# Two layers of a hybrid diffusion backbone on one core: activation slots and weight pieces that begin at other byte addresses

## The chip, the cores and the metric

One Trainium2 chip, one of its cores. The metric is the device time of one execution, in microseconds. The kernel before was run twice without a profile: 3562.77 and 3561.64 us, median 3562.2 us. One more execution was profiled; all durations below come from that one.

## The reference, cut to what matters

A latent stream x (1024 tokens, 1024 features) and a context prefix (256 tokens) go through two layers. Each layer does the following, in float32:

```
h  = modulate(rms_norm(x, g1), shift, scale)        # per token norm, per feature affine
qkv = h @ w_in                                      # 1024 -> three head groups A, B, C
o  = attention of the groups A (GQA), B (window), C (differential)
x  = x + gate1 * (o @ w_out)
h2 = modulate(rms_norm(x, g2), shift2, scale2)
u, g = split(dwconv3(h2 @ w_up))                    # 1024 -> 2 x 2816
x  = x + gate2 * ((silu(g) * u) @ w_down)
```

The context tokens take the same path with modulations of their own; the second layer computes only what the latent stream needs.

## The kernel before, in words

**Layout.** Features lie on the 128 partitions, tokens along the free dimension: 1280 tokens (1024 latent, 256 context) of a 128-feature block are one slot of 1280 float32 values, 5120 bytes per partition. There are eight blocks (KT = 8).

**Pairs of high and low parts.** Every large product is made of operands split in two: a high part, rounded to the format `fp32r` that TensorE takes in one pass (written `hh`, `ah`, `wh`, `iph`), and a low part, the rest (`hl`, `al`, `wl`, `ipl`). A product is three matmuls: high by high, high by low, low by high. `split` (L102 to L104) makes a pair: a cast on ACT and a subtraction on DVE.

**Slots.** One pool lives through the whole program: eight slots `x0` to `x7` for the residual stream and sixteen slots `hh0, hl0` to `hh7, hl7` for the normalised activations. `slot` (L295) hands them out by name. Two of them, `x7` and `hl7`, are eight values wider than used. Pools place tiles one behind the other, so the program as it is built puts `hh0` at byte 57504 of the partition and each further `h` slot 5120 bytes on; the weight pieces `w` of the FFN begin at byte 143008 and then every 4096. All sixteen `h` slots and all weight pieces so begin at 160 modulo 256; the `x` slots begin at 128 modulo 256. Every column offset that a matmul takes in them is a multiple of 512 bytes, or of 256 bytes in the windowed attention, so no moving operand of the program begins off a multiple of 32 bytes.

**Stages of a layer.**
- *Modulation* (`ada`, L170): `w_ada` streamed through free slots as the moving operand, 128x512 pieces. In the first layer the first piece goes through the `h` slots, later ones through the `x` slots.
- *First norm* (L241 to L278): the scaled input is cast to `hh` on ACT (L278), and `hl` is made on DVE (L267) or POOL (L264).
- *Input projection* (`inproj`, L398): here the `h` slots are the stationary operand, 128 tokens at a time, and the pieces `iph`, `ipl` of `w_in` are the moving operand, 384 wide. 60 steps of 24 matmuls.
- *Attention* (`attention`): the `h` slots are free then and hold queries, keys and bias tables. ACT or POOL write the high part (L585, L587), DVE or POOL the low part (L594). Scores (L672) read them as both operands. A list scheduler, `Sched`, sets the order at build time by costs that stand in the code; byte addresses do not enter it. The probabilities `P` are transposed (L776) and multiplied by the values (L795).
- *Output projection* (L927) and second norm: stationary are the pieces of `w_out`, moving are the `h` slots, 512 or 256 tokens at a time. The first three pieces of `w_out` lie in the FFN's weight buffers.
- *FFN*: up projection (`mm`, L991), stationary `w` (128 of the 1024 values of a piece), moving `hh` or `hl`, in chunks of 512, 512 and 256 tokens in the first layer and twice 512 in the second; down projection (`down_mm`, L1078), stationary `w`, moving the activation tiles `ah`, `al`. The weights come through `Stream`: the raw piece by DMA, split into a pair of tiles from `tiles` (L1499), three pairs in rotation (`n_hi` = 3).

Matmuls of these four products, by their lines: 2880 (L398), 1152 (L927), 5280 (L991), 2640 (L1078); the scores (L672) are 1536.

Of the kernel before, what the change touches and what calls it, by code (L numbers as in the profile page):

```python
# [15 lines left out]
F32R = mybir.dt.float32r  # L16
# [6 lines left out]
L, D, T, NL, NC = 2, 1024, 1280, 1024, 256  # L23
# [50 lines left out]
class Build:  # L74
# [218 lines left out]


    def slot(self, s, dt=F32):  # L295
        w = T + 8 if s in ("x7", "hl7") else T
        return self.sl[1].tile([128, w], dt, name=self.name(s), tag=s, bufs=1)[:, :T]

    def new_h(self):
        return [(self.slot(f"hh{k}", F32R), self.slot(f"hl{k}", F32R)) for k in range(KT)]  # L300
# [1186 lines left out]
class Stream:  # L1487
# [9 lines left out]
        return self.raws.tile([128, 1024], F32, name=self.kb.name("wr"), tag="wr", bufs=self.n_raw)  # L1497

    def tiles(self):  # L1499
        return tuple(self.pool.tile([128, 1024], F32R, name=self.kb.name("w"), tag=f"w{z}", bufs=self.n_hi) for z in "hl")  # L1500

    def ahead(self, loads, splits):
        kb, nc = self.kb, self.kb.nc
# [119 lines left out]
```

## Time and profile before

| What | Value |
|---|---|
| median of the two runs | 3562.2 us |
| the profiled execution's own time | 3566.8 us |
| its span, first to last instruction | 3565.0 us |
| mean granted TensorE clock in it | 0.985 of full speed |
| PE, PE weight loads, DVE, ACT, POOL busy | 96%, 82%, 58%, 41%, 29% |
| data moved by DMA | 251.4 MB, 71 GB/s on average |

The profiled execution is 4.6 us (0.13%) longer than the median, and 1.8 us of it lie outside the span. In the profile, a matmul's time is its whole passage through the array, so two matmuls that follow each other overlap; the pace is read from one start to the next, or from the length of a run of matmuls divided by their count. `PE` is the matmul, `PEld` the load of its stationary operand. In a row such as `psu<-hh,w`, `psu` is the PSUM tile that is written, and the names behind the arrow are the operands.

### The profile page before, as it was taken

How to read it: one execution, taken by the hardware profiler on the slowest of the kernel's cores; microseconds unless marked ns; L12 is line 12 of the kernel's file. 1: busy time of each engine (PE TensorE's matmuls, PEld its weight loads, DVE VectorE, ACT ScalarE, POOL GpSimd, SP SyncE). 2: the span in 40 equal slices, each digit the busy share in tenths (PEclk: the TensorE clock that was granted, in tenths of full speed). 3: DMA queues.
4: the chain of work that ended last, by engine and by line, in shares of the span. 5: the costliest groups of instructions: out<-in, count | busy, mean ns of one | idle time of the engine just before them, and what ended most of it. 6: DMA issues, size and time to landing. Idle time of an engine off the chain costs nothing.

```text
span 3565.0 us, 55714 instructions
## 1 busy us (share of the span) xinstructions
PE 3412.1 (96%) x21808; PEld 2921.6 (82%) x21808; DVE 2082.9 (58%) x4535; ACT 1447.6 (41%) x2501; POOL 1022.7 (29%) x874
## 2 busy tenths in 40 slices
PE   6999898999999999999999899899999999999999
PEld 3779787788888888888887789788888888888887
DVE  5533578877464455444546644578976555455555
ACT  4322587778442122212123322587876322222221
POOL 3434567757110000000002344577854200000000
PEclk8999999999999999999999999999999999999999
DMA  5553321210211111111112452312201111111112
GB/s 208 169 203 114 102 53 45 78 31 21 88 44 42 36 38 40 42 42 36 42 34 95 135 173 80 96 49 54 80 27 53 61 48 48 48 48 54 42 48 77
DMA packets 116070, 251.39 MB, mean 71 GB/s; under 512 B 13664, under 2 KB 55136, under 8 KB 115808
## 3 DMA queue, kind: packets, MB, share of 16 engines
q1 hardware_dynamic: 75600, 225.02, 19.7%
q10 hardware_dynamic: 40208, 22.81, 2.1%
q8 instruction: 172, 2.82, 0.3%
q14 instruction: 90, 0.74, 0.1%
HBM read 216.85 MB, written 30.93 MB: 70 GB/s over the span
## 4 chain that ended last, share of the span: by engine, by line
PE 82%; DVE 8%; DMA 3%; ACT 2%; issue 2%; POOL 2%; SPq 0%; ACTq 0%; DVEq 0%; POOLq 0%
PE psu L991 15%; PE psg L991 15%; PE dacc L1078 15%; PE acc L398 11%; PE T L795 7%; PE T L776 6%; PE acc L927 4%; PE S L672 4%; DVE P L688 3%; PE T L672 2%; PE ada L170 1%; DMA x<-in_wada 1%; DVE hl L267 1%; DVE hh L594 1%; ACT P L715 1%
## 5 line engine op out<-in xcount | busy, mean ns | idle before, releaser
L1085 DVE SCALAR_TENSOR_TENSOR x<-dacc,mods,x 128x512 f32<-128x512 f32 (+1 forms) x440 | 303.6, 696 | 474.9 <-PE dacc L1078 474.8
L1078 PE MATMUL dacc<-ah,w 128*128 128x512 f32 (+1 forms) x1760 | 530.4, 369 | 2.1 <-DVE x L1085 1.6
L991 PE MATMUL psu<-hh,w 128*128 128x512 f32 (+1 forms) x1760 | 516.5, 368 | 1.1 <-ACT hh L278 1.1
L991 PE MATMUL psg<-hh,w 128*128 128x512 f32 (+1 forms) x1760 | 516.4, 368 | 0.0
L715 ACT ACTIVATE P<-P,sm 128x1280 f32<-128x1280 f32 (+3 forms) x360 | 435.2, 1210 | 117.7 <-DVE sm L705 71.3
L103 ACT CAST w<-wr 128x1024 fp32r<-128x1024 f32 x138 | 144.1, 1044 | 725.8 <-PE psg L991 538.5
L1078 PEld LDWEIGHTS dacc<-ah,w 128*128 128x128 f32 x1760 | 322.0, 188 | 60.9 <-DVE x L1085 4.6
L991 PEld LDWEIGHTS psu<-hh,w 128*128 128x128 f32 x1760 | 321.4, 189 | 56.7 <-ACT hh L278 1.3
L991 PEld LDWEIGHTS psg<-hh,w 128*128 128x128 f32 x1760 | 321.4, 189 | 55.7
L398 PE MATMUL acc<-iph,hh 128*128 128x384 f32 (+1 forms) x960 | 336.3, 350 | 5.7 <-ACT iph L103 3.9
L398 PE MATMUL acc<-iph,hl 128*128 128x384 f32 (+1 forms) x960 | 324.6, 338 | 8.7 <-DVE hl L267 5.1
L776 PE MATMUL T<-ident,P 128*128 128x128 f32 x2400 | 316.5, 276 | 16.4 <-DVE sm L688 7.0
L398 PE MATMUL acc<-ipl,hh 128*128 128x384 f32 (+1 forms) x960 | 324.3, 338 | 1.1 <-DVE ipl L104 1.1
L991 PE MATMUL psu<-hl,w 128*128 128x512 f32 (+1 forms) x880 | 324.7, 369 | 0.1
L1078 PE MATMUL dacc<-al,w 128*128 128x512 f32 (+1 forms) x880 | 324.4, 369 | 0.0
L991 PE MATMUL psg<-hl,w 128*128 128x512 f32 (+1 forms) x880 | 324.0, 368 | 0.0
L688 DVE CUSTOM_DVE_ANT_0 P<-S,small 128x1024 f32<-128x1024 f32 x256 | 311.9, 1218 | 18.8 <-PE S L672 18.6
L776 PEld LDWEIGHTS T<-ident,P 128*128 128x128 f32 x2400 | 271.9, 141 | 52.6 <-issue 9.0
L723 POOL TENSOR_SCALAR P<-P,sm 128x1280 f32<-128x1280 f32 (+3 forms) x216 | 262.8, 1219 | 164.3 <-DVE sm L718 141.0
L781 ACT COPY PT<-T 128x512 f32<-128x512 f32 (+1 forms) x529 | 279.3, 586 | 62.4 <-PE T L776 61.3
L795 PE MATMUL T<-PT,v 128*64 128x128 f32 x4800 | 296.5, 278 | 3.1 <-DVE sm L688 1.4
L795 PEld LDWEIGHTS T<-PT,v 128*64 128x64 f32 x4800 | 262.4, 138 | 35.5 <-issue 13.3
(195 smaller groups left out, 5794.4 us busy)
## 6 DMA issues: line engine op xcount, KB each, us to landing
wr<-in_wup SPq DMA_DIRECT2D x88, 512.0 KB, 3.5
x<-in_wada SPq DMA_DIRECT2D x80, 512.0 KB, 6.6
wr<-in_wdown SPq DMA_DIRECT2D x44, 512.0 KB, 3.5
ipr<-in_win SPq DMA_DIRECT2D x48, 384.0 KB, 3.8
qs<-sg ACTq DMA_DIRECT2D x108, 128.0 KB, 1.8
raw<-qs SPq DMA_DIRECT2D x40, 320.0 KB, 4.7
raw<-qs SPq DMA_DIRECT2D x72, 160.0 KB, 3.1
v<-vs SPq DMA_DIRECT2D x30, 320.0 KB, 3.3
```

The lines of the kernel that those rows point to most:

```text
L103: self.nc.scalar.copy(hi, raw)
L398: nc.tensor.matmul(acc[:, c0:], lhsT=a[:, o:o + 128], rhs=b[:, k % 2, c0:], start=(k == 0 and a is hi and b is wh), stop=(k == KT - 1 and ...
L672: nc.tensor.matmul(S[:, pc:pc + w], lhsT=q[:K, 128 * t:128 * t + 128], rhs=k[:K, k0:k0 + w], start=(j == 0), stop=(j == len(ks) - 1))
L688: nc.vector.tensor_tensor_reduce(P[:, o:o + n], S[:, base:base + n], tab, op0=ALU.add, op1=ALU.max, scale=1.0, scalar=-3e38, accum_out=sm[ ...
L715: nc.scalar.activation(P[:, :n], P[:, :n], AF.Exp, bias=sm[:, 0:1], scale=1.0, accum_out=sm[:, 1:2])
L723: lambda e: nc.gpsimd.tensor_scalar(P[:, :n], P[:, :n], sm[:, 2:3], 1.0, op0=ALU.mult, op1=ALU.mult),
L776: nc.tensor.transpose(tp[:, 256 * x + 128 * hs:256 * x + 128 * hs + 128], P[hs][:, col[kt]:col[kt] + 128], self.ident[:])
L781: nc.scalar.copy(ts[:, :w], tp[:, :w])
L795: nc.tensor.matmul(O[64 * hs:64 * hs + 64, :128], lhsT=hds[hs]["v"][:, kt, :], rhs=ts[:, x + 128 * hs:x + 128 * hs + 128], start=(kt == kt ...
L991: nc.tensor.matmul(ps[:, o:o + n], lhsT=a[:, 128 * k:128 * k + 128], rhs=b, start=(k == 0 and a is wh and b is hi), stop=(k == KT - 1 and ...
L1078: nc.tensor.matmul(acc, lhsT=a[:, off:off + 128], rhs=b[:, o:o + n], start=(kk == 0 and a is wh and b is hi), stop=(kk == 1 and a is wl))
L1085: nc.vector.scalar_tensor_tensor(xs, acc, self.mods[l][:, 40 + m, v:v + 1], xs, op0=ALU.mult, op1=ALU.add)
```

## The change

`slot` and `tiles` now hand out a window into a wider tile. An `h` slot is 1288 values wide, and its 1280 values begin 0 to 7 values (0 to 28 bytes) into the tile: `hh` of block k at 2k modulo 8, `hl` at 2k + 1 modulo 8. So `hh0` begins at +0 bytes, `hl0` at +4, `hh1` at +8, `hl1` at +12, and so on to `hl3` at +28, and again from `hh4` on. A weight tile is 1032 values wide, and its 1024 values begin at +16, +32 or +0 bytes, one of the three for each pair in rotation. The slot `hl7` keeps its width, `x7` too.

```
     def slot(self, s, dt=F32):
-        w = T + 8 if s in ("x7", "hl7") else T
-        return self.sl[1].tile([128, w], dt, name=self.name(s), tag=s, bufs=1)[:, :T]
+        if s[0] == "x":
+            return self.sl[1].tile([128, T + 8 if s == "x7" else T], dt, name=self.name(s), tag=s, bufs=1)[:, :T]
+        o = (2 * int(s[2:]) + (s[1] == "l")) % 8
+        return self.sl[1].tile([128, T + 8], dt, name=self.name(s), tag=s, bufs=1)[:, o:o + T]
...
     def tiles(self):
-        return tuple(self.pool.tile([128, 1024], F32R, name=self.kb.name("w"), tag=f"w{z}", bufs=self.n_hi) for z in "hl")
+        self.nt = o = (getattr(self, "nt", 0) + 4) % 12
+        return tuple(self.pool.tile([128, 1032], F32R, name=self.kb.name("w"), tag=f"w{z}", bufs=self.n_hi)[:, o:o + 1024]
+                     for z in "hl")
```

Fifteen slots grow by 32 bytes, so the tiles behind them in the partition move up by 480 bytes, and those behind the weight tiles by up to 672. Tiles that are handed out from the far end of the partition stay where they are, and nothing runs out of room.

On all five engines the instructions, their shapes and their order are the same, row by row. Only what four of them wait for differs, because tiles that share memory with earlier ones now overlap others: two multiplications of `P` on POOL (L723, one at each attention's start) name two more DMA queues each, and two loads at the boundary of the layers (L348, L326) name one engine less each.

In the program as it is built, the moving operand of 3520 of the 5280 matmuls of L991, of 768 of the 1152 of L927 and of 918 of the 1536 of L672 now begins 4, 8 or 12 bytes past a multiple of 16; before, of none. The stationary operand does so in 1920 of the 2880 of L398. The stationary operands of L991 and L1078 stay on multiples of 16 bytes.

## Prediction

> **What bounds the kernel now.** I read the page first: the busy shares, then the chain of work that ended last.
>
> ```profile
> span 3565.0 us, 55714 instructions
> PE 3412.1 (96%) x21808; PEld 2921.6 (82%) x21808; DVE 2082.9 (58%) x4535; ACT 1447.6 (41%) x2501; POOL 1022.7 (29%) x874
> PE 82%; DVE 8%; DMA 3%; ACT 2%; issue 2%; POOL 2%; SPq 0%; ACTq 0%; DVEq 0%; POOLq 0%
> PE psu L991 15%; PE psg L991 15%; PE dacc L1078 15%; PE acc L398 11%; PE T L795 7%; PE T L776 6%; PE acc L927 4%; PE S L672 4%; DVE P L688 3%; PE T L672 2%; PE ada L170 1%; DMA x<-in_wada 1%; DVE hl L267 1%; DVE hh L594 1%; ACT P L715 1%
> ```
>
> TensorE carries 82% of the chain, and 45% of it are the FFN's matmuls. The change adds and removes no instruction and moves none, so it can act only through the duration of single instructions. The question is therefore what sets the pace of a matmul. Next I took the chain in order of time, for long runs of matmuls without a break:
>
> ```profile
> 1057.34 13.78 PE psu L991 x72
> 1071.12 13.78 PE psg L991 x72
> 1664.50 13.78 PE psu L991 x72
> 2863.93 10.88 PE psu L991 x48
> 2885.69 10.88 PE psu L991 x48
> 3484.09 10.88 PE psg L991 x48
> 162.55 4.17 PE acc L398 x24
> ```
>
> A run of 72 is 48 matmuls of 512 columns and 24 of 256; a run of 48 is 512 columns throughout. So 512 columns take 10.88 / 48 = 226.7 ns, and 256 columns (13.78 - 10.88) / 24 = 120.8 ns. The slope is 105.8 / 256 = 0.413 ns per column, and 226.7 - 512 x 0.413 = 15.0 ns are left as a fixed part of every matmul. The third width bears this out: 15.0 + 384 x 0.413 = 173.8 ns, and the run of 24 in L398 gives 4.17 / 24 = 173.8 ns. Nothing waits in these runs: each reads all eight high and all eight low slots, with weights from one of three pairs of buffers, and the lengths agree to 0.01 us from 1057 to 3495 us.
>
> **The moving operand.** What would a start 4, 8 or 12 bytes past a multiple of 16 do? No matmul of the trace has one, so I bound it. The nearest row on another engine is DVE's, in the depthwise convolution:
>
> ```profile
> L977 DVE SCALAR_TENSOR_TENSOR tu<-psu,cw,tu 128x1023 f32<-128x1023 f32 x44 | 56.3, 1278 | 68.7 <-ACT tu L974 68.7
> L981 DVE SCALAR_TENSOR_TENSOR tu<-psu,cw,tu 128x1023 f32<-128x1023 f32 x44 | 56.1, 1276 | 0.5
> ```
>
> L977 reads and writes `tu` from its second value on, 4 bytes past the tile's start, and its PSUM operand from the first; L981 has it the other way round. 1278 against 1276 ns: for DVE it does not matter which operand is 4 bytes off. The nearest row on TensorE is a step of 32 bytes, in the scores of the first head pairs:
>
> ```profile
> L672 PE MATMUL S<-x,x x128: 387/397/796, 390.8 to 2308.5; 128*128 128x512 f32 x128
> L672 PE MATMUL S<-x,hh x64: 390/396/504, 439.8 to 2376.6; 128*128 128x512 f32 x64
> L672 PE MATMUL S<-x,hl x64: 387/396/776, 515.6 to 2441.9; 128*128 128x512 f32 x64
> ```
>
> In the first row both operands lie in `x` slots and begin at 128 modulo 256; in the others the stationary one lies in an `h` slot, at 160 modulo 256. The medians are 397, 396 and 396 ns: whether the two operands begin at the same place of a 64-byte block changes nothing.
>
> Lower bound: 0. A gain by other starts would have to come out of the 15.0 ns, and is a rival below. Upper bound for an orderly memory: one more group of four columns per matmul whose start is off 16 bytes, 4 x 0.413 = 1.65 ns. There are 3520 + 768 + 918 = 5206 such matmuls, so 8.6 us. I take 2 us, near the lower end, because both neighbouring rows show nothing.
>
> [...]
>
> **The stationary operand.** In L398, 1920 of 2880 stationary operands come off 16 bytes, and the FFN's move by 16 or 32 bytes only. The load of one lies under the previous matmul's stream. How much room it has, the smallest loads show:
>
> ```profile
> L776 PEld LDWEIGHTS T<-ident,P 128*128 128x128 f32 x2400 | 271.9, 141 | 52.6 <-issue 9.0 <-DVE sm L688 8.2 <-DVE PT L783 6.4
> L398 PEld LDWEIGHTS acc<-iph,hl 128*128 128x128 f32 x960 | 184.8, 193 | 10.5 <-DVE hl L267 6.4 <-POOL hl L264 4.1
> ```
>
> The 2400 loads of the transposes keep TensorE busy 271.9 us, 113 ns each; in L398 a matmul starts only every 173.8 ns, so a load could take 60 ns longer before it showed. I take 0. If that cover did not hold and a shifted load cost four column times, it would be 1920 x 1.65 = 3.2 us.
>
> **DMA into shifted slots.** Only the first modulation loads large pieces into `h` slots at a time when somebody waits:
>
> ```profile
> 26.36 1.03 PE L170 MATMUL ada<-hh,sil 128*2 128x512 f32 x4 [0.25 <-DMA hh<-in_wada]
> 27.64 1.03 PE L170 MATMUL ada<-hl,sil 128*2 128x512 f32 x4 [0.25 <-DMA hl<-in_wada]
> hh<-in_wada SPq DMA_DIRECT2D x8, 512.0 KB, 9.9
> hl<-in_wada SPq DMA_DIRECT2D x8, 512.0 KB, 10.2
> ```
>
> A piece arrives every 1.28 us (27.64 - 26.36), 410 GB/s. Each row of it is 4096 bytes, so a ragged edge is under 1% of it, 0.1 us over twelve shifted pieces. Even at twice the time per shifted piece it would be 12 x 1.28 = 15 us. I take 0, because the rows are long. The bias tables that go into `h` slots later are loaded ahead of the head pair that uses them.
>
> **ACT, DVE and POOL on shifted slots.** DVE is settled by L977 and L981. POOL writes `hl` in the first norm and in attention:
>
> ```profile
> L264 POOL TENSOR_TENSOR hl<-x,hh 128x256 fp32r<-128x256 f32 x20 | 15.2, 764 | 32.0 <-ACT hh L276 32.0
> PE acc L398 <- POOL hl L264: 3.6, 1, 3.6
> L594 POOL TENSOR_TENSOR hl<-raw,hl 32x1280 fp32r<-32x1280 f32 x7 | 20.5, 2927 | 1.4 <-POOL P L723 0.9
> ```
>
> TensorE waits for POOL once in the first norm, 3.6 us; at twice the time the 20 pieces of L264 would add at most their own 15.2 us, and the attention's share has DVE and ACT beside it. ACT casts into `hh` are the same kind of unit-step stream as DVE's. I take 0 for the three together and keep +15 us as the upper end.
>
> **The four waits.** The two multiplications on POOL wait for more queues, but what those queues carried are raw pieces of `w_in`, which the input projection has used up before; what POOL waits for there is DVE:
>
> ```profile
> 399.08 1.35 POOL L723 TENSOR_SCALAR P<-P,sm 128x1280 f32<-128x1280 f32 x1 [1.05 <-DVE sm L718]
> 1896.00 1.76 SPq L348 DMA_DIRECT2D ipr<-in_win  x4
> 1955.08 34.91 SPq L348 DMA_DIRECT2D ipr<-in_win  x6
> ```
>
> The load at the layers' boundary is issued at 1896 us. The next ones wait until its buffers have been split, and come at 1955 us, so there are some 60 us of room. Cost and gain 0.
>
> **Sum.** 2 + 0 + 0 + 0 + 0 = +2 us, with ends at 0 and 8.6 + 3.2 + 15 + 15 = +42 us. Against the profiled execution (3566.8 us) that is 3569 us; it stands 4.6 us above the median of the runs, and the forecast is for the median: 3562.2 + 2 = **3564 us**. Its own range is 3555 to 3604, the lower end by the spread between executions.
>
> **Rival 1, slower: shifted streams run below pace.** [...] For it: one column every 0.413 ns is four bytes per partition in that time, against 1278 / 1023 = 1.25 ns per value on DVE, so DVE's indifference says little about a stream three times as fast. [...] The price from which it decides is 71 us (2%) / 5206 = 13.7 ns, or 33 columns per shifted matmul.
>
> **Rival 2, faster: the 15.0 ns are a clash between the streams.** [...] If that is because all starts agree, and other starts end it where they differ modulo 16 (3520 in L991, 768 in L927, 1920 in L398), it saves 6208 x 15.0 = 93 us: **3469 us**. Against it: the fixed part is the same for 256, 384 and 512 columns, though the load meets another part of the stream in each, and the same for `x` and `h` operands.
>
> [...]
>
> **Rival 3: it does not shift what it says.** The built program has the offsets in the operands, by the counts above, so I give this nothing.
>
> **How the numbers follow.** The forecast with its small terms, within 2% (about what a measurement of this kernel can tell from no change): 0.72. Rival 1 at any price above 13.7 ns: 0.21, a third of it below 3720. Rival 2: 0.07. The range leaves out rival 2 and the dear part of rival 1: 3550 to 3720, which holds 0.71 + 0.07 = 0.78.
>
> **What would show it.** Right: the runs of 72 and 48 in L991 stay at 13.78 and 10.88 us, and those of 24 in L398 at 4.17. [...] Rival 2: L991 and L398 both shrink. A shorter or longer first 35 us would point to DMA, a longer L594 or L264 to POOL. The forecast is wrong if a shifted matmul's pace moves by more than 13.7 ns.

## The result and the profile after

The changed kernel took 3595.3 us (median of two runs, 3594.8 and 3595.8), the kernel before 3562.2. The ratio is 1.0092, with a 95% interval from 1.0067 to 1.0116: 33 us, 0.9% slower, and less than 2%. The forecast was 3564 us. One execution of run 11 below took 6747.6 us, nearly twice the others, and is left out of that run's time and ratio; why it was slow is not known. The line numbers from L298 on are two higher in the changed kernel (L991 is now L993, L1078 is L1080, L398 is L400).

First the page of the changed kernel: span, busy times, and the chain that ended last, by engine.

```profile
span 3594.0 us, 55715 instructions
PE 3450.4 (96%) x21808; PEld 2931.5 (82%) x21808; DVE 2079.2 (58%) x4535; ACT 1447.1 (40%) x2501; POOL 1016.4 (28%) x874
PE 83%; DVE 8%; DMA 3%; ACT 2%; issue 2%; POOL 2%; SPq 0%; ACTq 0%; DVEq 0%; POOLq 0%
```

The counts on the five engines are the same, and DVE, ACT and POOL are not busier. TensorE is 38.3 us busier (3450.4 - 3412.1) and the span is 29.0 us longer. To see where, I cut both spans at the FFN of layer 1 and of layer 2 (first matmul of the up projection to last of the down projection). Two of the four windows of before:

```profile
1028.70:1949.10 920.40, 916.66 (x4785) 787.89 (x4784) 467.51 (x593) 202.23 (x196) 18.10 (x22) 1.00 0.13 42
2838.00:3560.80 722.80, 721.36 (x3177) 594.80 (x3176) 371.70 (x390) 166.77 (x162) 0.71 (x1) 1.00 0.15 51
```

and the same two of the changed kernel (the length comes after the window's bounds, then busy time and count of PE, PEld, DVE, ACT, POOL, then the granted clock, the DMA share and GB/s):

```profile
1030.10:1964.30 934.20, 930.38 (x4785) 788.88 (x4784) 467.62 (x594) 202.37 (x196) 18.22 (x22) 1.00 0.12 42
2848.30:3589.80 741.50, 740.06 (x3177) 596.54 (x3176) 371.90 (x390) 166.67 (x162) 0.71 (x1) 1.00 0.15 49
```

The same matmuls at the same granted clock take 13.8 us longer in layer 1's FFN and 18.7 us in layer 2's, 32.5 us together. The stages outside sum to 3.5 us less. They vary from one execution to the next, also where nothing in them was touched: in runs 10 to 12 below, which share layer 1, its up projection (the chain's first `PE psu L991 x24`) starts at 1023.1, 1024.5 and 1019.2 us. So nothing is read from the 3.5. All of the slowdown that shows in the span is in the FFN. Two other products slowed too, by less than those stages vary: the 576 matmuls of 512 columns in L927 went from 227.4 to 232.7 ns (3 us), the 2880 of 384 columns in L398 from 174.2 to 175.6 ns (4 us). The chain in order of time shows the form of the loss:

```profile
162.02 4.21 PE acc L400 x24
1059.26 14.07 PE psu L993 x72
1073.33 13.99 PE psg L993 x72
2874.60 11.21 PE psu L993 x48
2885.81 11.09 PE psg L993 x48
3533.81 11.22 PE psg L993 x48
3553.74 36.50 PE dacc L1080 x156
```

The runs that were 13.78 and 10.88 us are now 13.99 to 14.07 and 11.09 to 11.22. The last run of the down projection, whose operands all begin on 16 bytes, went from 35.88 us to 36.50:

```profile
3525.34 35.88 PE dacc L1078 x156
```

Start to start, the mean of 512 columns rose from 227.1 to 233.1 ns in L991 (4224 matmuls of that width) and from 227.7 to 231.7 ns in L1078 (2112): 4224 x 6.0 + 2112 x 4.0 = 33.8 us. The 256-column matmuls got faster by 0.4 and 1.3 ns (1056 and 528 of them), 1.1 us. That leaves 32.7 us, against 32.5 in the windows. So the loss is 4 to 6 ns on the mean of the wide matmuls of both lines, and no stall anywhere.

### The profile page after: what moved, and what is told of

It is laid out like the page before. It is cut to its first block, busy times and chain, and to the rows that moved or that the text cites. A ratio compares the mean times of both kernels' runs of the same rounds, so it can differ in the third digit from the quotient of the medians.

```text
span 3594.0 us, 55715 instructions
## 1 busy us (share of the span) xinstructions
PE 3450.4 (96%) x21808; PEld 2931.5 (82%) x21808; DVE 2079.2 (58%) x4535; ACT 1447.1 (40%) x2501; POOL 1016.4 (28%) x874
## 4 chain that ended last, share of the span: by engine, by line
PE 83%; DVE 8%; DMA 3%; ACT 2%; issue 2%; POOL 2%; SPq 0%; ACTq 0%; DVEq 0%; POOLq 0%
PE psu L993 15%; PE psg L993 15%; PE dacc L1080 14%; PE acc L400 11%; PE T L797 7%; PE T L778 6%; PE acc L929 5%; PE S L674 4%; DVE P L690 3%; PE T L674 2%; PE ada L170 1%; DMA x<-in_wada 1%; DVE hh L596 1%; PE pt L466 1%; DMA hh<-in_wada 1%
## 5 line engine op out<-in xcount | busy, mean ns | idle before, releaser
L1080 PE MATMUL dacc<-ah,w 128*128 128x512 f32 (+1 forms) x1760 | 535.5, 372 | 2.2 <-DVE x L1087 1.6
L993 PE MATMUL psu<-hh,w 128*128 128x512 f32 (+1 forms) x1760 | 524.2, 372 | 1.1 <-ACT hh L278 1.1
L993 PE MATMUL psg<-hh,w 128*128 128x512 f32 (+1 forms) x1760 | 522.8, 372 | 0.0
L1080 PEld LDWEIGHTS dacc<-ah,w 128*128 128x128 f32 x1760 | 321.4, 188 | 66.4 <-DVE x L1087 4.5
L993 PEld LDWEIGHTS psu<-hh,w 128*128 128x128 f32 x1760 | 321.9, 189 | 63.8 <-ACT hh L278 1.3
L993 PEld LDWEIGHTS psg<-hh,w 128*128 128x128 f32 x1760 | 322.1, 189 | 63.2
L400 PE MATMUL acc<-iph,hh 128*128 128x384 f32 (+1 forms) x960 | 337.8, 352 | 5.6 <-ACT iph L103 3.7
L400 PE MATMUL acc<-iph,hl 128*128 128x384 f32 (+1 forms) x960 | 325.5, 339 | 8.7 <-DVE hl L267 5.2
L993 PE MATMUL psu<-hl,w 128*128 128x512 f32 (+1 forms) x880 | 329.0, 374 | 0.1
L993 PE MATMUL psg<-hl,w 128*128 128x512 f32 (+1 forms) x880 | 329.0, 374 | 0.0
L400 PE MATMUL acc<-ipl,hh 128*128 128x384 f32 (+1 forms) x960 | 327.1, 341 | 1.4 <-DVE ipl L104 1.4
L1080 PE MATMUL dacc<-al,w 128*128 128x512 f32 (+1 forms) x880 | 326.4, 371 | 0.0
```

What stands on the lines that cost most here:

```text
L400: nc.tensor.matmul(acc[:, c0:], lhsT=a[:, o:o + 128], rhs=b[:, k % 2, c0:], start=(k == 0 and a is hi and b is wh), stop=(k == KT - 1 and ...
L993: nc.tensor.matmul(ps[:, o:o + n], lhsT=a[:, 128 * k:128 * k + 128], rhs=b, start=(k == 0 and a is wh and b is hi), stop=(k == KT - 1 and ...
L1080: nc.tensor.matmul(acc, lhsT=a[:, off:off + 128], rhs=b[:, o:o + n], start=(kk == 0 and a is wh and b is hi), stop=(kk == 1 and a is wl))
```

## The experiments

The pace in this section is the mean from one matmul start to the next for 512 columns, breaks left out. Places are byte addresses modulo 256 in the built program, and the distance is the stationary operand's place less the moving one's. "In step" stands for the 226.7 ns of the kernel before.

| Run | Starts | us | ratio and interval | L991, ns | L1078, ns |
|---|---|---|---|---|---|
| kernel before | all 160 | 3562.2 | | 227.1 | 227.7 |
| changed kernel | as the change has them | 3595.3 | 1.0092 [1.0067, 1.0116] | 233.1 | 231.7 |
| 1 | weight pieces of the change alone | 3588.4 | 1.0073 [1.0056, 1.0090] | 232.5 | 231.1 |
| 2 | slots of the change alone | 3596.7 | 1.0092 [1.0077, 1.0108] | 234.2 | 227.5 |
| 3 | all on 32 bytes, steps of 64 | 3596.2 | 1.0093 [1.0078, 1.0108] | 232.8 | 231.9 |
| 4 | as 3, slots and weight pieces 4 bytes later | 3617.7 | 1.0154 [1.0139, 1.0169] | 236.7 | 232.7 |
| 5 | moving 160, stationary 128; L1078 all 128 | 3591.4 | 1.0076 [1.0061, 1.0091] | 233.4 | 229.7 |
| 6 | all 160, weight steps of 17 x 256 | 3562.1 | 0.9994 [0.9985, 1.0004] | 227.1 | 227.7 |
| 7 | as 6, weight pieces 4 bytes later | 3591.5 | 1.0078 [1.0063, 1.0093] | 232.4 | 232.4 |
| 8 | slots in steps of 32; L1078 all 128 | 3588.0 | 1.0075 [1.0058, 1.0092] | 232.3 | 229.2 |
| 9 | as 6, 13 distances in turn | 3585.6 | one run; before 3566.3 | by distance | by distance |
| 10 | as 6, layer 2's L991 all 164 | 3593.9 | 1.0097 [1.0079, 1.0115] | 237.7 | 232.3 |
| 11 | as 6, layer 2's L991 all 176 | 3576.2 | 1.0047 [1.0030, 1.0064] | 233.0 | 232.5 |
| 12 | as 6, layer 2's L991 and L1078 all 192 | 3561.3 | 1.0004 [0.9994, 1.0013] | 226.7 | 226.8 |

In runs 10 to 12 the two last columns are those of layer 2.

Three theories stood at the start. *Line*: a stream is slowed by its own start off 16 bytes (a line is here the author's unit of counting, from one multiple of 16 bytes to the next; no row shows a line of the memory). *Agreement*: the pace of 226.7 ns needs moving and stationary operand to begin at the same remainder of some larger power of two. *Place*: 160 modulo 256 is good by itself.

### Runs 1 and 2: the change in halves

Run 1 has only the windows of the weight pieces:

```
-        return tuple(self.pool.tile([128, 1024], ...) for z in "hl")
+        self.nt = o = (getattr(self, "nt", 0) + 4) % 12
+        return tuple(self.pool.tile([128, 1032], ...)[:, o:o + 1024] for z in "hl")
```

> Only the weight tiles of the FFN are shifted (windows at +16, +32, +0 bytes of tiles 32 bytes wider); the h slots are as before, so every moving operand of the FFN begins on a multiple of 32 bytes. Theory 'line': a stream is slowed by its own start off 16 bytes; then the runs of 48 matmuls of the up projection stay at 10.88 us and those of 72 at 13.78 us, the down projection stays at 226.7 ns a matmul, and the time at 3562 to 3566 us. Theory 'agreement': the pace of 226.7 ns holds only where the moving and the stationary operand begin at the same remainder of some power of two above 16 bytes, whichever of them is shifted; then the runs grow to about 11.1 to 11.2 us and 14.0 us, the down projection to about 231 ns as in the changed kernel, and the time to 3590 to 3600 us.

Run 2 has only `slot` of the change.

> Only the h slots are shifted as in the change; the weight tiles are as before, and all tiles behind the slots lie 480 bytes higher. In the down projection moving and stationary operands then begin at the same remainder of 256 bytes (128), in the up projection they do not. 'Line': up projection slow (runs of 48 at 11.2 us), down projection at 226.7 ns, time 3585 to 3595 us. 'Agreement': the same for both, runs of 48 at 11.1 to 11.25 us, down projection back at 226.7 ns, input projection still at about 175.6 ns instead of 173.8, time 3585 to 3592 us. A third theory, 'place' (the good remainder is 160 of 256, and no other will do), expects the down projection to stay slow, at about 231 ns, because both its operands now begin at 128.

Rows of the chain, first of run 1, then of run 2:

```profile
2880.64 11.20 PE psg L991 x48
3546.59 36.48 PE dacc L1078 x156
```

```profile
2879.04 11.25 PE psu L993 x48
3556.14 35.90 PE dacc L1080 x156
```

In run 1 the moving operands all lie at 160 in L991 and at 96 in L1078 (the activation tiles lie behind the weight tiles), none off 16 bytes, yet L991 and L1078, at 232.5 and 231.1 ns, lose nearly as much as with the whole change (233.1 and 231.7). *Line* can't be the main cause. In run 2 L991 loses (234.2 ns), and L1078, all at 128 there, is back at 35.90 us: *place* 160 is not what counts. Each half alone costs about what both do, 27 and 36 us over the kernel before in the same set of runs: they take away the same thing.

### Runs 3 and 4: on 32 bytes, and then 4 bytes off

Run 3 puts every `h` slot and weight piece at a multiple of 64 bytes behind a first one at 32 modulo 64, so that they agree modulo 64 but not modulo 256. In run 4 `o` is 1 in both places. To make room, `nsq` has one buffer here and in the runs from 6 on except 8; run 6 shows that this costs nothing.

```
+        h, o = s[0] == "h", 0
+        return self.sl[1].tile([128, T + 24 if s == "hl7" else T + 16 if h else T + 8 if s == "x7" else T], ...)[:, o * h:o * h + T]
...
+        o = 0
+        return tuple(self.pool.tile([128, 1056], ...)[:, o:o + 1024] for z in "hl")
```

> No start leaves the remainder 32 of 64 bytes: h slots 64 bytes wider (hl7 96), weight tiles 128 bytes wider, no window offset; hh and hl differ by 64 of 128, weight buffers by 128 of 256. To make room, the second norm's squares have one buffer instead of two. 'Line' and 'agreement' with a modulus of 64 or less: all paces as before (10.88 and 13.78 us, 226.7 ns, 173.8 ns), time 3562 to 3580 us with what the missing buffer costs. 'Agreement' with a modulus of 128 or 256: the matmuls with low parts, or with the weight buffers that are 128 off, are slow, runs of 48 at 11.0 us or more.

> The same as the kernel with steps of 64, but every h slot and every weight tile begins 4 bytes later. In the up projection both operands are then 4 bytes off a multiple of 32 and agree with each other; in the down projection only the stationary one is 4 bytes off, in the input projection too. 'Line': up projection slow (runs of 48 above 11.1 us), down projection and input projection at their old pace. 'Agreement': the up projection stays at 10.88 and 13.78 us, while the down projection goes to about 231 ns and the input projection to about 175 ns.

Run 3, then run 4:

```profile
2883.43 11.19 PE psg L991 x48
3550.74 36.63 PE dacc L1078 x156
```

```profile
2890.32 11.39 PE psu L991 x48
3577.01 36.70 PE dacc L1078 x156
```

Run 3 has no start off 32 bytes and is as slow as the change (3596.2 us, 232.8 ns in L991), so agreement modulo 64 is not enough. Agreement of single matmuls isn't either: in L1078 1680 of its 2640 have both operands at 160, with the others in between, and its mean is still 231.9 ns. Run 4 costs 21 us more: 3.9 ns a matmul in L991, where both operands moved off the line by the same 4 bytes, and 0.8 ns in L1078, where only the stationary one did (which also ends the agreement of those 1680, so this is no clean price). *Line* therefore exists as a second cost, shown by L991.

### Runs 5 to 8: which agreement

```
run 5  -        w = T + 8 if s in ("x7", "hl7") else T
       +        w = T + 8 if s in ("x7",) else T
run 6  +        return tuple(self.pool.tile([128, 1088], ...)[:, 0:1024] for z in "hl")
run 7  +        return tuple(self.pool.tile([128, 1088], ...)[:, 1:1025] for z in "hl")
run 8  +        w = T + 8 if s[0] == "h" or s == "x7" else T
```

> The kernel before with one slot narrower, so that all that lies behind the slots of h is 32 bytes lower: every moving operand of L991, L927 and L398 still begins at 160 modulo 256, every weight piece, wo, iph and ipl at 128, and ah, al and w of L1078 all at 128. All starts are on 16 bytes, and the distance from moving to stationary operand is the same 32 bytes in every matmul of the three lines. Agreement between moving and stationary operand: L991, L927 and L398 (counted as in the kernel before) fall out of step as in the slots-only run, 512 columns 231 to 234 ns in place of 227, runs of 48 in L991 11.1 us, 3583 to 3593 us; L1078 stays at 227.5. Agreement only among operands that follow one another in the same role (all moving ones alike, all stationary ones alike): 227 ns and 10.88 us everywhere, 3562 us. Line (each stream slowed by its own start off 16 bytes): 3562 us as well.

> The kernel before with weight pieces in steps of 4352 bytes (17 x 256) in place of 4096: every operand of the four lines still begins at 160 modulo 256, but weight buffers next to each other differ by 256 modulo 512. To make room one buffer of the norm's squares is gone. Agreement modulo 256 or less: 227 ns, runs of 48 at 10.88 us, 3562 us and what the missing buffer costs, up to 3566. Agreement modulo 512 or more: L991, L1078 and L927 at 231 to 233 ns, 11.1 us, 3585 to 3595 us, L398 (no weight piece) unchanged at 4.17 us for 24. Line: as before, 3562 to 3566 us.

> The run with weight pieces in steps of 17 x 256 bytes, with every weight piece's window 4 bytes later: stationary operands of L991 and L1078 at 164 modulo 256, moving ones at 160, all alike. Line, for the stationary operand alone: the price of a stationary start 4 bytes off 16 by itself, by the run with everything 4 bytes later about 1 ns per matmul of L1078 where moving operands stayed on 16, 5 to 10 us over that run. Agreement to the byte: 4 bytes apart is out of step, 231 to 234 ns in L991 and L1078, 3585 to 3597 us. Agreement to the line of 16 bytes, and no price for the stationary operand's own shift: the same time as that run.

> The slots-only half of the change with its stride and without its offsets: every slot of h is 32 bytes wider, so that their starts step through all eight multiples of 32 modulo 256, all on 16 bytes; weight pieces as in the kernel before but for their common place, 128 modulo 256, like ah and al. The slots-only run with its offsets of 4 to 28 bytes was 3596.7 us, 234.2 ns in L991. Agreement alone: L991 and L927 231 to 233 ns, L1078 227.5, 3582 to 3592 us; what is left to 3596.7 is the price of moving starts off 16 bytes, by the run with everything 4 bytes later 3 to 4 ns for each of the three quarters of them that are off. Line alone: 3562 us, L991 at 227 ns.

Chain rows of runs 5, 6, 7 and 8, in this order:

```profile
2877.81 11.20 PE psg L991 x48
3544.38 35.89 PE dacc L1078 x156
```

```profile
2858.97 10.88 PE psu L991 x48
3520.40 35.90 PE dacc L1078 x156
```

```profile
2872.37 11.16 PE psu L991 x48
3550.36 36.65 PE dacc L1078 x156
```

```profile
2868.07 11.15 PE psu L991 x48
3544.37 35.88 PE dacc L1078 x156
```

Run 5 moves everything behind the slots by 32 bytes, with no window and no start off 32, and that alone costs 28 us. It is agreement between the moving and the stationary operand that counts; all moving ones alike and all stationary ones alike doesn't help (233.4 ns in L991). Run 6 differs from the kernel before by 256 between neighbouring weight buffers and is as fast (3562.1 us): 256 is modulus enough. With run 3 (64 is not enough) it is 128 or 256; run 9 decides for 256. Run 7 shows that 4 bytes apart is already out of step (232.4 ns). In runs 5 and 8 L1078, all at 128 as in run 2, was expected at 227.5 ns and came to 229.7 and 229.2 on the mean. Its last 156 matmuls do have the old pace (35.89 and 35.88 us). But in layer 2 most of it comes twelve matmuls at a time between runs of L991, and in these two runs it takes seven or eight of the twelve to fall into step. In run 2, where L991 is out of step as well, it is in step from the first; what makes that difference isn't shown. Run 8 takes the offsets of 4 to 28 bytes out of run 2 and keeps slots in steps: L991 goes from 234.2 to 232.3 ns. The times, 3588.0 and 3596.7 us, have overlapping intervals, so the price of these offsets is read from the pace.

### Run 9: a scan of the distance

```
+        o = (0, 1, 2, 3, 4, 8, 12, 16, 20, 24, 32, 48, 60)[self.nt]
+        self.nt = (self.nt + 1) % 13
```

> A scan of the distance in one kernel: the run with weight pieces in steps of 17 x 256 bytes, where the pieces' windows begin in turn 0, 4, 8, 12, 16, 32, 48, 64, 80, 96, 128, 192 and 240 bytes into their buffers, both pieces of a pair alike; the moving operands all stay at 160 modulo 256. Each run of 48 in L991 (layer 2) has one distance throughout. To be read: the mean of 512 columns for each distance, run by run. Agreement to the byte: 226.7 ns at 0 alone (10.88 us a run), 231 to 234 ns (11.1 to 11.2 us) at every other distance, the 4 of the run before and the 32 of the kernel with a narrower slot among them. Agreement to the line of 16 bytes and an own price of a shifted stationary operand: 4, 8 and 12 bytes alike at 231 to 232, and 16, 48, 80 and 240 (whole lines) unlike them. A place or bank of 32 or 64 bytes: 226.7 again at 64, 128 and 192; this is unlikely, since in the run of everything in steps of 64 bytes L991 had 232.8. Whole run 3583 to 3592 us.

Runs of 48 from the chain, each with one weight piece and so one distance:

```profile
2957.03 10.90 PE psu L991 x48
2967.93 11.16 PE psg L991 x48
3023.59 11.20 PE psu L991 x48
3034.78 11.19 PE psg L991 x48
3101.48 10.91 PE psg L991 x48
3157.02 11.20 PE psu L991 x48
3224.10 10.99 PE psu L991 x48
3235.09 10.96 PE psg L991 x48
3290.37 11.20 PE psu L991 x48
3357.51 11.14 PE psu L991 x48
3490.68 11.23 PE psu L991 x48
3524.06 10.88 PE psg L991 x48
```

Their distances in bytes, in the same order: 0, 4, 48, 64, 0, 32, 192, 240, 16, 128, 96, 240. Over all records of L991:

```
distance   0     4     8     12    16    32    48    64    80    96    128   192   240
512 cols   227.7 232.4 230.5 232.3 233.3 233.2 233.2 233.2 231.8 234.1 232.4 229.0 228.0 ns
256 cols   119.5 118.0 116.4 117.2 118.4 118.0 118.1 116.7 118.8 117.3 119.3 116.7 117.4 ns
```

Only distance 0 has the old pace in all its runs of 48 (its mean holds the first matmuls after each break). A stationary operand that begins 16 or 64 bytes lower than the moving one (240, 192) is nearest, which no theory had expected, and the last row, at 240, has the old pace too: 10.88 us, where the other runs of 48 at 240 have 10.96. So 0 isn't the only distance at which the pace can occur; it is the one at which it always did. 128 is as slow as most others, which settles the modulus at 256. The old pace is also the best of the scan for 512 columns. For 256 columns it is the worst.

### Runs 10 to 12: agreement at another place

Layer 2 uses 1024 of a slot's 1280 values, so its windows may begin later without a wider slot. In run 10 the step is one value, in run 11 four, in run 12 eight; run 12 moves the activation tiles of L1078 along as well.

```
-            H = self.new_h()
+            H = [tuple(z[:, l:] for z in p) for p in self.new_h()]
...
+            self.lay = l
...
+        o = self.kb.lay
```

> The run with weight pieces in steps of 17 x 256 bytes, with layer 2's slots of h and its weight pieces both 4 bytes later: in layer 2's L991 both operands begin at 164 modulo 256, off the lines of 16 bytes and in full agreement; layer 1 is as before and serves as the control within the run. Layer 2's L1078 has moving operands at 160 and stationary ones at 164, the 4 bytes apart of an earlier run. Agreement alone: layer 2's L991 stays at 226.7 ns and 10.88 us a run of 48; L1078 of layer 2 goes to about 232 ns, 5 ns x 1056 = 5 us, and L927 of layer 2 loses up to 2 us: 3567 to 3571 us. Line as a cost of its own, also in agreement: L991 of layer 2 loses the 3 to 4 ns of the run with everything 4 bytes later, 230 to 231 ns, 11.06 us a run, 2112 x 4 = 8 us more: 3575 to 3579 us.

> As the run with layer 2's operands of L991 both 4 bytes later, with 16 bytes in place of 4: 176 modulo 256 in both, on the lines of 16 bytes and in agreement, another place than any so far. Agreement, with or without a cost of the line: 226.7 ns and 10.88 us in layer 2's L991; layer 2's L1078, 16 bytes apart, at 232 to 233 ns: 3567 to 3571 us. Place (only some starts allow the pace of 226.7): L991 of layer 2 off it, 3575 us and more.

> As the run with layer 2's operands of L991 both 16 bytes later, with 32 bytes in place of 16, and the operands of layer 2's L1078 moved along: both lines have both operands at 192 modulo 256 in layer 2; of that layer's L927 only the pieces from wo are 32 bytes apart. Starts on 32 bytes and in agreement (what 160 and 128 have and 176 lacks): L991 and L1078 of layer 2 fall into step at 226.7 ns after each break, 10.88 us a run of 48, and the whole is 3561 to 3566 us. Place 160, or 128 for L1078, alone: layer 2's L991 at 231 to 234 ns and its L1078 likewise, 3575 to 3585 us. Agreement of whatever start, and the run at 176 slow only because its L1078 was 16 bytes apart and handed its pace on: 226.7 ns here too, so this run does not tell that apart from the first; the starts of L991 after a break do, in the run at 176.

Chain rows of runs 10, 11 and 12:

```profile
2860.26 11.41 PE psu L991 x48
3548.74 36.65 PE dacc L1078 x156
```

```profile
2860.70 11.09 PE psu L991 x48
3017.03 11.20 PE psu L991 x48
3540.97 35.92 PE dacc L1078 x156
```

```profile
2854.92 10.88 PE psu L991 x48
3516.34 35.94 PE dacc L1078 x156
```

Run 12 did as agreement says. Run 11 did not: both operands at 176, on 16 bytes and in full agreement, and L991 is at 11.09 to 11.20 us. Agreement as I had put it failed here. What 160, 128 and 192 have and 176 lacks is a start on 32 bytes; other places were not tried. The pace at 176 was not handed on from L1078, which is 16 bytes apart in that run: L991 was off 227 ns from 2834.6 us on, and the layer's first L1078 comes at 2907.7. The four times of run 11 fall into two pairs, 3570.9 and 3571.9, 3580.5 and 3582.5 us; the trace is of the execution of 3582.5, so what the shorter pair did differently isn't shown. Run 10, at 164, lies another 4.7 ns a matmul above run 11 (237.7 against 233.0); at 3593.9 us it is dearer than both theories had it, 3567 to 3579.

How the pace settles after a break tells more than its mean. Successive intervals between matmul starts, in ns, from the traces:

```
before   L991, from 2838.0 us   233 236 228 233 231 226 227 227 226 227 227 226
run 12   L991, from 2829.1 us   232 231 227 227 226 227 227 226 227 227 226 227
run 11   L991, from 2834.6 us   232 228 232 228 232 228 232 228 232 228 232 228
run 5    L1078, after a run of L991 32 bytes apart
                                240 224 231 236 229 231 231 228 226 226 228 226
run 11   L1078, layer 2, 16 bytes apart, early
                                233 233 232 233 235 234 233 233 232 233 235 234
run 11   L1078, the last 156, 16 bytes apart too
                                233 232 226 227 227 226 227 227 226 227 227 226
```

The fast pace is something that a run of matmuls falls into, in these rows after two to seven of them, and then keeps. With equal starts on 32 bytes it did so after every break that I followed: in the kernel before, in run 6 and in run 12, each of the 45 unbroken stretches of more than twelve wide matmuls in L991 and L1078 has a mean of 227 ns from the ninth interval on. At 176 it stayed in other patterns, 228 and 232 in turn or 233. At 16 bytes apart the same operands ran in either pattern, depending on how the run had begun: that is why the last run of 156 is 35.92 us in run 11 while the shorter runs of L1078 before it were at 233. So distance and place make the fast pattern likely; they are not the pattern itself. What in the chip makes it, no run here shows.

No kernel of the twelve beats the one before by more than its interval.

## Why the prediction was right, and where it was wrong

The verdict of the forecast was right (within 2%), and its own range, 3555 to 3604, holds 3595. The cause and the size were not: its first sign of being right, runs of 72 and 48 that stay at 13.78 and 10.88 us, did not come, and that the time stayed within the range was luck, as the terms below show.

**What bounds the kernel** held: the FFN's runs carry the difference, and the pace of a matmul is what changed.

**The step that failed is the stationary operand, taken at 0.** I reasoned that its load lies under the previous matmul's stream with some 60 ns to spare, and that moves by 16 or 32 bytes are harmless. Run 1, where only the weight pieces have windows, costs 27 us. Loads did not get longer, as these rows of the loads before and after show:

```profile
L991 PEld LDWEIGHTS psu<-hh,w 128*128 128x128 f32 x1760 | 321.4, 189 | 56.7 <-ACT hh L278 1.3
L993 PEld LDWEIGHTS psu<-hh,w 128*128 128x128 f32 x1760 | 321.9, 189 | 63.8 <-ACT hh L278 1.3
```

The room I measured was room for one load's length, but what cost time was the distance between the two operands' starts (run 5: 32 bytes, 233.4 ns in L991), which no row of one operand alone could show. Two smaller slips stand beside it. The weight pieces did not move by 16 or 32 bytes only: with the slots ahead of them wider by 480 bytes, they begin at 0, 64, 144, 160, 224 and 240 modulo 256 in L991. And the 60 ns came from the transposes' loads; L398's own row, shown under it, has 193 ns a load, more than the 173.8 ns from start to start, so that room doesn't follow from it. L398's pace grew by 1.4 ns on the mean, 4.0 us over its 2880 matmuls where I had 3.2 as the upper end, and not by starts off 16 bytes: run 8, which has none, has the same 175.6 ns.

**The row that led me there** was L672: 397, 396 and 396 ns, whether its operands were at 128 and 128 or at 128 and 160. From this I said that the relation of the two places changes nothing. But those scores come three or four wide ones at a time between breaks (start to start 337, 236, 228, then a transpose; 339, 231, 236, then a transpose), 233.1 ns on average before and 232.8 after, intervals over 300 ns left out. That is the length over which a run of L991 is still settling (two to seven matmuls in the rows above), so they are hardly ever in step, though 1136 of the 1536 have both operands at 160, and had no pace to lose. The nearest row was one of another regime; the 226.7 ns of L991, next to the 233.1 of L672 for the same 512 columns, stood in the trace and should have made me ask. The recorded durations say the same. L991 before and after the change:

```profile
L991 PE MATMUL psu<-hh,w 128*128 128x512 f32 x1408 | 450.4, 390 | 1.1 <-ACT hh L278 1.1
L993 PE MATMUL psu<-hh,w 128*128 128x512 f32 x1408 | 458.2, 395 | 1.1 <-ACT hh L278 1.1
```

The 396 and 397 ns of L672 were the durations of matmuls out of step already.

**The moving operand**, +2 us with 8.6 as its upper end: the slots alone cost 36 us. Most of it is agreement again, not the shift: run 8, whose slots step by 32 bytes, has 232.3 ns against run 2's 234.2. The shift's own price, run 2 against run 8, is 1.9 ns as a mean over matmuls of which two thirds are shifted (3520 of 5280; the expectation of run 8 says three quarters), some 2.8 ns for each, against 1.65 as my upper end and 0.4 as the value I took. It is an estimate: the two runs also differ a little in their distances. No run shows the one more group of four columns, 1.65 ns, from which the 8.6 us here and the 3.2 us of the stationary operand were made. In its place run 4 has 3.9 ns a matmul over run 3 in L991, with both operands 4 bytes off 16.

By the 16 bytes at which I counted shifted starts, 176 should do as well as 160; no row of before showed that size. Runs 11 and 12 have steps of 16 and 32 bytes (11.09 to 11.20 us a run of 48, against 10.88), so at the places tried the measurement goes by 32.

**DMA, ACT, DVE and POOL**, taken at 0, show nothing. The input projection starts at 37.5 us where it started at 38.0, so the first pieces were no slower. DVE's convolution and POOL's low parts after the change, by group:

```profile
L979 DVE SCALAR_TENSOR_TENSOR tu<-psu,cw,tu 128x1023 f32<-128x1023 f32 x44 | 56.3, 1279 | 76.1 <-ACT tu L976 76.1
L264 POOL TENSOR_TENSOR hl<-x,hh 128x256 fp32r<-128x256 f32 x20 | 14.8, 742 | 32.0 <-ACT hh L276 32.0
```

1279 ns where it was 1278, and 742 for POOL's writes into shifted slots where it was 764. The two ends of 15 us for them were never used; it is only because they stood in the sum that its upper end, +42, covered a +33 from elsewhere. The four waits cost nothing that shows.

**Rival 1** put the cost on shifted moving streams. The runs of 48 grew by 0.2 to 0.3 us, 4 to 7 ns a matmul, and L1078 slowed too (231.7 ns from 227.7) though its moving operands stayed on 16 bytes. A price off 16 bytes shows, but it is 2.8 ns (run 2 against run 8, the estimate above), 3.9 (run 4 against run 3) and 4.7 (run 10 against run 11), far from the 13.7 at which that rival decided.

**Rival 2** had the right variable and the wrong sign. It asked whether the 15.0 ns were there because all starts agree, and would go if they differed. They are at their least for 512 columns, of all starts tried, because all starts agree: no mean in the table is below 226.7 ns.

## What to carry to other kernels

When wide matmuls follow each other without a break, look at where both operands begin, modulo 256 and on 32 bytes: here equal starts in both layers were worth 24 to 36 us of 3562 (runs 1 to 3, 5, 7 and 8), and in run 5 one tile made 32 bytes narrower ahead of the others lost 28 of them. Compare the pace of one shape at several places of the program before taking a row as a bound: two values for the same shape (226.7 and 233.1 ns) say that there are two regimes, and a row from the slower one can't show what is lost by leaving the faster. A cost that lies in the relation of two operands isn't found by bounding each operand by itself.

## What the runs showed that was not expected

- The pace has memory: the same operands at the same addresses ran at 227 and at 233 ns in one execution (run 11, L1078).
- The sign depends on the width. Out of step, 512 columns lose 5 to 6 ns in L991, 256 columns gain up to 3 (119.5 to 116.4 ns in the scan; but 121.2 in run 4, with both operands off the line), and 384 columns move little (174.2 before; 173.9 in run 5, where they were 32 bytes apart; 175.6 after the change; 176.6 in run 4). A kernel of 256-column matmuls might want unequal starts; that was not tried.
- In the scan, a stationary operand that begins 16 or 64 bytes lower than the moving one costs 0.3 to 1.3 ns, one that begins as much higher costs 5.5 (228.0 and 229.0 against 233.3 and 233.2 ns, from 227.7).
